# Readout tables among the chunk inputs, six weight halves on another engine, regrouped adaLN columns: one S5/convolution layer on one core

## The chip, the core and the metric

The kernel runs on one core of one Trainium2 chip. The metric is the device time of one execution in microseconds (us); a smaller one is better. Engines are named as in the profile: PE is TensorE (matmuls), DVE is VectorE, ACT is ScalarE, POOL is GpSimd, and SP is the queue that issues most DMAs.

## The reference, cut to what matters

One layer over 1024 latent tokens with 1024 channels and a prefix of 256 context tokens. adaLN gives shift, scale and gate vectors (six of 1024 channels). Two token mixers run side by side, a bidirectional diagonal state space model (S5) with a GLU, and a short gated convolution; they are merged by sigmoid gates. A gated MLP with a 3x3 depthwise convolution follows.

```python
h  = modulate(rmsnorm(x, norm1_g), sh1, sc1)
p  = h @ w_in
y_a = s5_branch(p[..., :512], pc[..., :512], ...)      # scan over chunks, readout, then z * sigmoid(z @ glu_w + glu_b)
y_b = b_gate * depthwise_conv1d(c_gate * x_val, sconv_w)
merged = gate_a * (y_a @ proj_a) + gate_b * (y_b @ proj_b)
x  = x + g1 * (merged @ w_out)
h2 = modulate(rmsnorm(x, norm2_g), sh2, sc2)
x  = x + g2 * conv_ffn(h2, ...)
```

## The kernel before

Matmuls in float32 precision are made of three passes: each operand is split in a high half (a ScalarE copy, `whi`, `ybh`, `woh`) and a low half (a subtraction, `wlo`, `ybl`, `wol`), and `mm3` adds three products (lines 211 to 213). `weight` (line 190) loads a 128x1024 block into `raw` (two buffers), makes `whi` on ScalarE (line 199) and `wlo` on VectorE, or on the engine given in `lo_eng` (line 202); whi and wlo have two buffers each. PSUM has two buffers of 128x1024 for such matmuls (`mm`) and a few small ones (`ax`).

The S5 branch works on 160 chunks of 8 tokens (32 of the context, 128 latent), in 32 groups, eight to a block m:
- `chunk_inputs(m)` (line 617) loads U and multiplies it by the tables W1 into the states XS, with three ScalarE copies for each of six small PSUM tiles. Then level 0 of the scan is done for block m, in three parts (`advance`, line 587, four VectorE steps a part at lines 603 to 606). Its temporaries lie in the pool bp, on the right side of SBUF.
- `build_w2(sb)` (line 631) makes one of eight readout tables of four groups: six VectorE steps (lines 637 to 642) into W2 (one buffer), two DMAs to Yd (line 644), four ScalarE copies into Bk, eight matmuls (`ax_K`, line 651) and a copy to Kt (line 653).
- `kernel_table` (line 655) makes the diagonal part K0 (matmuls at line 660, a VectorE step at line 662), writes Kt and K0 to Kd (lines 665, 666, 669), and copies Kd into Yd with 16 DMAs (line 672).
- `chunk_scan` (line 608) does levels 1 to 4 upwards, then the top, then levels 4 to 0 downwards, for groups 0 to 15 and then 16 to 31, on VectorE.
- `readout(sb)`, 16 of them: loads of `wt`, copies S of XS on ScalarE and VectorE (lines 786, 787), matmuls (lines 790 to 792), a gelu and DMAs to Zd.

The convolution: `conv_unit` for m = 0 to 3 with three `gate_matmul` each (mm_c, mm_x, mm_b, 48 matmuls each). The product of c and x goes to `cx` (one buffer), the three taps to `cv` (one buffer; lines 701 to 703), times mm_b (line 708), then the split to `ybh`, `ybl` in the pool yp. yp is opened on the right side when the pools bp and tb are closed (after line 740).

Then `branch_b(d)` for d = 0 to 7: gate 24 + d (48 matmuls, mm_gb, sigmoid at line 812), a projection (24 matmuls, mm_pb) and their product on VectorE (line 820). For d = 0 to 3 the readouts are issued between (0, 6, 6 and 4); before d = 4 the pool of XS is closed. From d = 4 on, three adaLN columns follow each branch: `mod_cols(n)` (line 845) loads 128 rows of 1024 and does one dot product on VectorE (line 849). Then z, gate 16, four GLU projections, the split to y_a, and branch a: gates 17 to 23 and proj_a (mm_ga, mm_pa; sigmoid at line 812, product at line 913), with the other twenty columns between, five for each of d = 1 to 4. `load_wout(k)` (line 897) loads a block of w_out into a `raw` buffer, multiplies it by g1b on GpSimd (line 900), and splits it.

What sets the order: the program's order is only a priority. Each engine's instructions are put in order when the kernel is built, by a simulated timeline of the program; on the chip each engine and each queue then goes strictly in that order. SBUF of a closed pool can be used again when its last reader is done. `issue_after` puts an instruction behind a given one on the same engine, as in

```python
    def held(eng):
        ins = hold.get(eng)
        return tc.issue_after(ins.ins) if ins is not None else nullcontext()
```

Of the kernel before, what the change touches and what calls it, by code (L numbers as in the profile page):

```python
# [22 lines left out]
P = 128  # L23
# [132 lines left out]
def layer_kernel(es: ExitStack, tc, I, out):  # L156
# [451 lines left out]
    def chunk_scan(gs, t1, t2, cap):  # L608

        for lv in range(1, NLV):  # L610
            advance(gs, lv, (2 << lv) - 1, t1, t2, cap)
        for c in range((2 << NLV) - 1, NC - 1, 1 << NLV):
            advance(slice(gs.start, gs.stop), NLV, c, t1, t2, cap, c)
        for lv in reversed(range(NLV)):
            advance(gs, lv, NCC - 1 + (1 << lv), t1, t2, cap, NC - 2)
# [15 lines left out]
    def build_w2(sb):  # L631
        g0 = sb * 4
        W2 = kp2.tile([P, 4, 2, L, H], F32, name=f"W2_{g0}", tag="W2")
        tmp = kp2.tile([P, 4, L, H], F32, name=f"W2t_{g0}", tag="W2t")
        e = [tview(E2[i], g0, 4) for i in range(2)]
        eng = dve
        eng.tensor_tensor(W2[:, :, 0], e[0], bview(Cr, g0, 4), op=ALU.mult)
        eng.tensor_tensor(tmp, e[1], bview(nCi, g0, 4), op=ALU.mult)
        eng.tensor_tensor(W2[:, :, 0], W2[:, :, 0], tmp, op=ALU.add)
        eng.tensor_tensor(W2[:, :, 1], e[0], bview(nCi, g0, 4), op=ALU.mult)  # L640
        eng.tensor_tensor(tmp, e[1], bview(Cr, g0, 4), op=ALU.mult)
        eng.tensor_tensor(W2[:, :, 1], W2[:, :, 1], tmp, op=ALU.subtract)
        for q in range(2):
            sync.dma_start(Yd[2 * sb + q][:, :, 0:2, :], W2[:, 2 * q:2 * q + 2].rearrange("p g r l h -> p g r (l h)"))
        pk = ax_tile([P, P], f"K{sb}")
        for i, b in enumerate((Br2, Bi2)):
            act.activation(Bk[i][0:64, :, 0:H], b[0:64, g0:g0 + 4], AF.Copy)
            act.activation(Bk[i][64:128, :, H:2 * H], b[64:128, g0:g0 + 4], AF.Copy)
        for g in range(4):
            for i in range(2):  # L650
                pe.matmul(pk[32 * g:32 * g + 32, :], Bk[i][:, g, :], W2[:, g, i].rearrange("p l h -> p (l h)"),
                          start=(i == 0), stop=(i == 1))
        act.activation(Kt[:, sb, :], pk, AF.Copy)

    def kernel_table():
        for m in range(MS):
# [5 lines left out]
            dve.scalar_tensor_tensor(K0[:, m, :], ident, dsk[:, m:m + 1], pk, op0=ALU.mult, op1=ALU.add)  # L662
        for q in range(4):
# [3 lines left out]
        for q in range(8):  # L667
            kg = Kd.rearrange("(m q) h i o -> q h m (i o)", q=8)[q]
            sync.dma_start(kg[:, :, 7 * H:8 * H], K0[16 * q:16 * q + 16, :, 16 * q:16 * q + 16])
# [61 lines left out]

    for m in range(MS):
        chunk_inputs(m)
        if m + 2 < MS:
            build_w1(2 * m + 4)
            build_w1(2 * m + 5)
        for g0, n in ((0, 3), (3, 3), (6, 2)):
            t1, t2 = (bp.tile([P, 512], F32, name=f"q{i}_{m}_{g0}", tag=f"T1_{i}") for i in range(2))
            advance(slice(8 * m + g0, 8 * m + g0 + n), 0, 1, t1, t2, 512)
    hold.clear()  # L740
# [4 lines left out]
    for sb in range(8):  # L745
        build_w2(sb)
# [7 lines left out]
    for gq in range(2):  # L754
        t1, t2 = (qp.tile([P, SEQ], F32, name=f"q{i}{gq}", tag=f"q{i}") for i in range(2))
        chunk_scan(slice(16 * gq, 16 * gq + 16), t1, t2, SEQ)
# [52 lines left out]
    def gate(m, key):  # L809
        psg = gate_matmul(m, key, pool_e)  # L810
# [4 lines left out]
    def branch_b(d):  # L815
        sg = gate(24 + d, f"gb{d}")
        if d % 2 == 0:
            conv["pw"] = weight(I["proj_b"][d // 2], pool_e)
# [33 lines left out]
    for d in range(MA, KT):  # L852
        branch_b(d)
        for n in range(3):
            mod_cols(16 + (d - MA) * 3 + n)
# [16 lines left out]
    sgd = {0: gate(16, "ga0")}  # L872
    for m in range(MS):
# [23 lines left out]
    def load_wout(k, src):  # L897
        raw = wp.tile([P, D], F32, name=f"raw_o{k}", tag="raw", bufs=2)
        sync.dma_start(raw, I["w_out"][k * P:(k + 1) * P, :])
        pool_e.tensor_tensor(raw, raw, g1b, op=ALU.mult)  # L900
# [5 lines left out]
    for d in range(KT):  # L906
# [8 lines left out]
        for n in range(28 + 5 * (d - 1), min(48, 28 + 5 * d)) if d else ():  # L915
            mod_cols(n)
# [277 lines left out]
```

## Time and profile before

| | us |
|---|---|
| median of 3 runs (lowest, highest) | 1476.52 (1476.14, 1478.03) |
| profiled execution | 1478.21 |
| span in its profile | 1476.4 |

| engine | busy us | share of the span |
|---|---|---|
| PE | 1401.2 | 95% |
| DVE | 973.5 | 66% |
| ACT | 539.6 | 37% |
| POOL | 508.0 | 34% |

A group's row names line, engine, operation, output <- input, shapes and count. A wait names the engine and line that waited and the instruction that ended the wait, as the profile infers it: if the named one had long been done, it was another, often a DMA. A start time is in us from the start of the span. Starts of neighbouring matmuls show their pace better than their durations, which overlap.

### The profile page before, as it was taken

To read this page: it belongs to the slowest core of one execution; us is meant where nothing else is said; L and a number is where in the kernel's file an instruction comes from. 1 tells how busy PE (TensorE), PEld (TensorE's weight loads), DVE (VectorE), ACT (ScalarE), POOL (GpSimd) and SP (SyncE) were. 2 spreads that over 40 slices of the span, in tenths; PEclk is the share of its full clock that TensorE was granted. 3 is DMA by queue.
4 is the path that set the end of the run, shared out by engine and by line. 5 is a ranking of instruction groups with operands and counts; after the bars stand their busy time and mean duration, and the time that the engine had idled before them with its cause. 6 is when DMAs were issued, how large, how long until landed. Compare 5 with 4: busy or idle time off the path is not lost. (4 is left out here: it accounts for less than half of the span.)

```text
span 1476.4 us, 16962 instructions
## 1 busy us (share of the span) xinstructions
PE 1401.2 (95%) x6488; PEld 1144.8 (78%) x6488; DVE 973.5 (66%) x1427; ACT 539.6 (37%) x760; POOL 508.0 (34%) x220
## 2 busy tenths in 40 slices
PE   6999978979999989999999999999999999998997
PEld 4787856768877767778878888888888887887885
DVE  6865789992143665037658878778787787349554
ACT  5645762215523411125433333323323342424332
POOL 0000000111123334550035554654555555645453
PEclk9999988989999998999999999999999999999999
DMA  9513211246674265133211111111111115434331
GB/s 327 196 50 95 78 41 60 78 114 184 210 206 117 79 213 142 58 106 122 87 42 51 43 57 44 47 54 44 57 43 44 57 45 191 140 96 141 109 107 57
DMA packets 82577, 148.71 MB, mean 101 GB/s; under 512 B 22336, under 2 KB 51264, under 8 KB 82496
## 3 DMA queue, kind: packets, MB, share of 16 engines
q1 hardware_dynamic: 79616, 137.90, 30.3%
q10 hardware_dynamic: 2880, 9.73, 1.9%
q8 instruction: 51, 0.84, 0.2%
q14 instruction: 30, 0.25, 0.0%
HBM read 129.80 MB, written 19.90 MB: 101 GB/s over the span
## 5 line engine op out<-in xcount | busy, mean ns | idle before, releaser
L202 POOL TENSOR_TENSOR wlo<-raw,whi 128x1024 fp32r<-128x1024 f32 x114 | 293.1, 2575 | 741.7 <-ACT whi L199 587.8
L1034 DVE SCALAR_TENSOR_TENSOR acc<-mm_up,cw,acc 128x945 f32<-128x945 f32 (+2 forms) x308 | 375.0, 1222 | 100.3 <-POOL acc L1026 91.5
L199 ACT ACTIVATE whi<-raw 128x1024 fp32r<-128x1024 f32 x126 | 133.6, 1060 | 499.6 <-issue 167.8
L213 PE MATMUL mm_up<-h2hi,wlo 128*128 128x512 f32 x704 | 273.8, 389 | 0.5 <-POOL wlo L202 0.5
L212 PE MATMUL mm_up<-h2lo,whi 128*128 128x512 f32 x704 | 274.0, 389 | 0.0
L211 PE MATMUL mm_up<-h2hi,whi 128*128 128x512 f32 x704 | 273.5, 389 | 0.4 <-DVE h2hi L969 0.4
L213 PEld LDWEIGHTS mm_up<-h2hi,wlo 128*128 128x128 f32 x704 | 132.2, 188 | 28.4 <-POOL wlo L202 0.9
L211 PEld LDWEIGHTS mm_up<-h2hi,whi 128*128 128x128 f32 x704 | 132.1, 188 | 28.0 <-DVE h2hi L969 0.7
L212 PEld LDWEIGHTS mm_up<-h2lo,whi 128*128 128x128 f32 x704 | 132.2, 188 | 27.3
L211 PE MATMUL mm_dn<-whi,fhd 128*128 128x512 f32 x308 | 119.5, 392 | 6.0 <-DVE x1r L1122 4.5
L212 PE MATMUL mm_dn<-wlo,fhd 128*128 128x512 f32 x308 | 120.7, 392 | 2.5 <-POOL wlo L202 2.5
L213 PE MATMUL mm_dn<-whi,fld 128*128 128x512 f32 x308 | 120.2, 391 | 0.0
L1026 POOL TENSOR_TENSOR acc<-acc,side 128x960 f32<-128x960 f32 x44 | 100.5, 2283 | 0.0
L207 DVE TENSOR_TENSOR fld<-f,fhd 128x512 fp32r<-128x512 f32 x44 | 57.6, 1323 | 53.5 <-ACT fhd L206 53.5
L849 DVE CUSTOM_DVE_ANT_0 mw<-mw,sc 128x1024 f32<-128x1024 f32 x32 | 54.1, 1699 | 47.1 <-DMA mw<-in_mod_wT_dram 42.5
L211 PEld LDWEIGHTS mm_dn<-whi,fhd 128*128 128x128 f32 x308 | 58.2, 189 | 18.9 <-DVE x1r L1122 4.9
L212 PEld LDWEIGHTS mm_dn<-wlo,fhd 128*128 128x128 f32 x308 | 58.3, 189 | 15.6 <-POOL wlo L202 3.5
L213 PEld LDWEIGHTS mm_dn<-whi,fld 128*128 128x128 f32 x308 | 58.2, 189 | 11.9
L196 DVE TENSOR_TENSOR raw<-raw,g2b 128x1024 f32<-128x1024 f32 x22 | 44.4, 2016 | 32.6 <-DMA raw<-in_ffn_w_down_dram 32.6
L211 PE MATMUL mm_ga<-hhi,whi 128*128 128x512 f32 x128 | 51.1, 400 | 11.4 <-ACT whi L199 11.4
L211 PE MATMUL mm_gb<-hhi,whi 128*128 128x512 f32 x128 | 51.6, 403 | 7.7 <-ACT sggb L812 7.7
L1045 POOL TENSOR_TENSOR f<-f,acc 128x1024 f32<-128x1024 f32 x22 | 53.4, 2426 | 10.1 <-DVE acc L1034 10.1
(323 smaller groups left out, 2655.7 us busy)
## 6 DMA issues: line engine op xcount, KB each, us to landing
raw<-in_ffn_w_up_dram SPq DMA_DIRECT2D x44, 512.0 KB
raw<-in_ffn_w_down_dram SPq DMA_DIRECT2D x44, 512.0 KB
mw<-in_mod_wT_dram SPq DMA_DIRECT2D x32, 512.0 KB
raw<-in_w_in_dram SPq DMA_DIRECT2D x28, 512.0 KB
wt<-Yd SPq DMA_DIRECT2D x16, 384.0 KB
mt<-in_mod_wT_dram SPq DMA_DIRECT2D x8, 512.0 KB
mn<-in_mod_nat_dram SPq DMA_DIRECT2D x8, 512.0 KB
Yd<-W SPq DMA_DIRECT2D x16, 256.0 KB
```

The source lines that it names most:

```text
L196: dve.tensor_tensor(raw, raw, scale, op=ALU.mult)
L199: act.activation(hi, raw, AF.Copy)
L202: (lo_eng or dve).tensor_tensor(lo, raw, hi.bitcast(F32), op=ALU.subtract)
L207: return dve.tensor_tensor(lo, src, hi.bitcast(F32), op=ALU.subtract)
L211: pe.matmul(ps, lh, rh, start=first, stop=False)
L212: pe.matmul(ps, lh, rl, start=False, stop=False)
L213: pe.matmul(ps, ll, rh, start=False, stop=last)
L849: dve.tensor_tensor_reduce(out=mw, in0=mw, in1=sc2, scale=1.0, scalar=0.0, op0=ALU.mult, op1=ALU.add, accum_out=modc[:, n:n + 1])
L1026: pool_e.tensor_tensor(acc[:, 1:, :], acc[:, 1:, :], side[:, 1:, :], op=ALU.add)
L1034: dve.scalar_tensor_tensor(acc[:, r0:r1, c0:c1], u[:, r0 + dr:r1 + dr, c0 + dc:c1 + dc], cw[:, m, i:i + 1], acc[:, r0:r1, c0:c1], op0=ALU. ...
L1045: pool_e.tensor_tensor(f[k], f[k], v, op=ALU.mult)
```

## The change

The diagonal table comes first, ahead of the chunk inputs. The tables 0 to 3 are built behind the chunk inputs of blocks 0 to 3, their matmuls one block later; tables 4 to 7 follow. Level 0 is done with the chunk inputs for blocks 0 and 1 only, and in `chunk_scan` for groups 16 to 31. Every step of the scan is put behind the last VectorE step of table 4. `hold` keeps its other entries, of instructions long issued by then. The low halves of gates 24 to 27 and of proj_b 0 and 1 are made on VectorE instead of GpSimd. The 32 adaLN columns are 9 behind branch b, 6 behind gate 16 and 17 in branch a, instead of 12 and 20. For w_out blocks 0 to 2, `raw` is a tile beside g1b, and the product is on VectorE.

```diff
@@ -605,9 +605,9 @@
             dve.tensor_tensor(dst, dst, a1, op=ALU.add)
             dve.tensor_tensor(dst, dst, a2, op=ALU.add)
 
-    def chunk_scan(gs, t1, t2, cap):
-
-        for lv in range(1, NLV):
+    def chunk_scan(gs, lv0, t1, t2, cap):
+
+        for lv in range(lv0, NLV):
             advance(gs, lv, (2 << lv) - 1, t1, t2, cap)
         for c in range((2 << NLV) - 1, NC - 1, 1 << NLV):
             advance(slice(gs.start, gs.stop), NLV, c, t1, t2, cap, c)
@@ -639,9 +639,13 @@
         eng.tensor_tensor(W2[:, :, 0], W2[:, :, 0], tmp, op=ALU.add)
         eng.tensor_tensor(W2[:, :, 1], e[0], bview(nCi, g0, 4), op=ALU.mult)
         eng.tensor_tensor(tmp, e[1], bview(Cr, g0, 4), op=ALU.mult)
-        eng.tensor_tensor(W2[:, :, 1], W2[:, :, 1], tmp, op=ALU.subtract)
+        hold[f"w2{sb}"] = eng.tensor_tensor(W2[:, :, 1], W2[:, :, 1], tmp, op=ALU.subtract)
         for q in range(2):
             sync.dma_start(Yd[2 * sb + q][:, :, 0:2, :], W2[:, 2 * q:2 * q + 2].rearrange("p g r l h -> p g r (l h)"))
+        return lambda: inner_table(sb, W2)
+
+    def inner_table(sb, W2):
+        g0 = sb * 4
         pk = ax_tile([P, P], f"K{sb}")
         for i, b in enumerate((Br2, Bi2)):
             act.activation(Bk[i][0:64, :, 0:H], b[0:64, g0:g0 + 4], AF.Copy)
@@ -652,7 +656,7 @@
                           start=(i == 0), stop=(i == 1))
         act.activation(Kt[:, sb, :], pk, AF.Copy)
 
-    def kernel_table():
+    def diagonal_table():
         for m in range(MS):
             pk = ax_tile([P, P], f"K0{m}")
             gs = slice(8 * m, 8 * m + 8)
@@ -660,13 +664,15 @@
                 pe.matmul(pk, b[:, gs, :].rearrange("p g h -> p (g h)"), cc[:, gs, :].rearrange("p g h -> p (g h)"),
                           start=(i == 0), stop=(i == 1))
             dve.scalar_tensor_tensor(K0[:, m, :], ident, dsk[:, m:m + 1], pk, op0=ALU.mult, op1=ALU.add)
+        for q in range(8):
+            kg = Kd.rearrange("(m q) h i o -> q h m (i o)", q=8)[q]
+            sync.dma_start(kg[:, :, 7 * H:8 * H], K0[16 * q:16 * q + 16, :, 16 * q:16 * q + 16])
+
+    def kernel_table():
         for q in range(4):
             kg = Kd.rearrange("(s q) h i o -> q h s (i o)", q=4)[q]
             sync.dma_start(kg[:, :, 8 * H:15 * H], Kt[32 * q:32 * q + 16, :, 0:7 * H])
             sync.dma_start(kg[:, :, 0:7 * H], Kt[32 * q + 16:32 * q + 32, :, H:8 * H])
-        for q in range(8):
-            kg = Kd.rearrange("(m q) h i o -> q h m (i o)", q=8)[q]
-            sync.dma_start(kg[:, :, 7 * H:8 * H], K0[16 * q:16 * q + 16, :, 16 * q:16 * q + 16])
         for j in range(L):
             for q in range(2):
                 sync.dma_start(Yd.rearrange("s (h j) q w o -> j q w s h o", j=L)[j, q, 2],
@@ -729,21 +735,28 @@
     for t in Bk:
         pool_e.memset(t, 0.0)
 
+    diagonal_table()
+    late = None
     for m in range(MS):
         chunk_inputs(m)
+        if late:
+            late()
         if m + 2 < MS:
             build_w1(2 * m + 4)
             build_w1(2 * m + 5)
-        for g0, n in ((0, 3), (3, 3), (6, 2)):
+        late = build_w2(m)
+        for g0, n in ((0, 3), (3, 3), (6, 2)) if m < 2 else ():
             t1, t2 = (bp.tile([P, 512], F32, name=f"q{i}_{m}_{g0}", tag=f"T1_{i}") for i in range(2))
             advance(slice(8 * m + g0, 8 * m + g0 + n), 0, 1, t1, t2, 512)
-    hold.clear()
+    hold.pop("dve")
     es_w.close()
     es_t.close()
     es_m = ExitStack()
     yp = pool("yp", stack=es_m, side="right")
-    for sb in range(8):
-        build_w2(sb)
+    for sb in range(MS, 8):
+        late()
+        late = build_w2(sb)
+    late()
     kernel_table()
     es_k2.close()
     es_u.close()
@@ -753,7 +766,8 @@
     qp = pool("qp", stack=es_q)
     for gq in range(2):
         t1, t2 = (qp.tile([P, SEQ], F32, name=f"q{i}{gq}", tag=f"q{i}") for i in range(2))
-        chunk_scan(slice(16 * gq, 16 * gq + 16), t1, t2, SEQ)
+        with held("w24"):
+            chunk_scan(slice(16 * gq, 16 * gq + 16), 1 - gq, t1, t2, SEQ)
     es_q.close()
 
     def ytile(key, m):
@@ -807,7 +821,7 @@
         return ps
 
     def gate(m, key):
-        psg = gate_matmul(m, key, pool_e)
+        psg = gate_matmul(m, key, None if 24 <= m < 28 else pool_e)
         sg = sgp.tile([P, SEQ], F32, name=f"sg{key}", tag="sg")
         act.activation(sg, psg, AF.Sigmoid)
         return sg
@@ -815,7 +829,7 @@
     def branch_b(d):
         sg = gate(24 + d, f"gb{d}")
         if d % 2 == 0:
-            conv["pw"] = weight(I["proj_b"][d // 2], pool_e)
+            conv["pw"] = weight(I["proj_b"][d // 2], None if d < 4 else pool_e)
         psp = proj_matmul(conv["pw"], d % 2, yb[0], yb[1], f"pb{d}")
         dve.tensor_tensor(mb[d], psp, sg, op=ALU.mult)
 
@@ -851,8 +865,8 @@
 
     for d in range(MA, KT):
         branch_b(d)
-        for n in range(3):
-            mod_cols(16 + (d - MA) * 3 + n)
+        for n in range(16 + 9 * (d - MA) // MA, 16 + 9 * (d - MA + 1) // MA):
+            mod_cols(n)
     es_ps.close()
     mm_order.insert(0, pool("ps_mm1", space=PSUM))
     es_ps = ExitStack()
@@ -870,6 +884,9 @@
 
     zh, zl = ysplit("z")
     sgd = {0: gate(16, "ga0")}
+    NM = 16 + 9 + 6
+    for n in range(16 + 9, NM):
+        mod_cols(n)
     for m in range(MS):
         if m % 2 == 0:
             wt = weight(I["glu_w"][m // 2], pool_e)
@@ -895,9 +912,10 @@
     wout = []
 
     def load_wout(k, src):
-        raw = wp.tile([P, D], F32, name=f"raw_o{k}", tag="raw", bufs=2)
+        raw = (wo.tile([P, D], F32, name=f"raw_o{k}", tag="xr", bufs=2) if k < 3 else
+               wp.tile([P, D], F32, name=f"raw_o{k}", tag="raw", bufs=2))
         sync.dma_start(raw, I["w_out"][k * P:(k + 1) * P, :])
-        pool_e.tensor_tensor(raw, raw, g1b, op=ALU.mult)
+        (dve if k < 3 else pool_e).tensor_tensor(raw, raw, g1b, op=ALU.mult)
         hi, lo = (src.tile([P, D], F32R, name=f"wo{t}{k}", 
                           **({"tag": "sg"} if src is sgp else {"tag": f"y{t}{k % MS}", "bufs": 1})) for t in ("h", "l"))
         split(hi, lo, raw)
@@ -912,7 +930,7 @@
         sg = sgd.pop(d)
         dve.tensor_tensor(sg, ps, sg, op=ALU.mult)
         pool_e.tensor_tensor(mb[d], mb[d], sg, op=ALU.add)
-        for n in range(28 + 5 * (d - 1), min(48, 28 + 5 * d)) if d else ():
+        for n in range(NM + 5 * (d - 1), min(48, NM + 5 * d)) if d else ():
             mod_cols(n)
         if 2 <= d < 4:
             load_wout(d - 2, wo)
```

## Rows read from the trace of the kernel before

**Rows 1.** Waits of PE, whole span: waiting line <- what ended it: us, times, longest.
```profile
PE mm_ga L211 <- ACT whi L199: 11.4, 2, 8.0
PE ax_K L651 <- DVE W L639: 8.9, 1, 8.9
PE mm_gb L211 <- ACT sggb L812: 7.7, 1, 7.7
...
PE ax_K L651 <- ACT whi L199: 5.0, 1, 5.0
...
PE mm_pb L211 <- DVE mb L820: 2.6, 1, 2.6
```

**Rows 2.** Windows by stage: busy us of each engine, granted clock, DMA share, GB/s.
```profile
core 0: us, PE busy (x) PEld busy (x) DVE busy (x) ACT busy (x) POOL busy (x), PEclk, DMA share, GB/s
125.00:203.50 78.50, 76.69 (x418) 65.69 (x417) 55.04 (x84) 57.63 (x92) 0.00 (x0) 1.00 0.23 70
203.50:226.00 22.50, 8.51 (x48) 6.31 (x48) 22.50 (x33) 9.15 (x20) 0.00 (x0) 0.71 0.23 70
203.50:330.00 126.50, 104.79 (x518) 81.04 (x518) 121.57 (x190) 30.79 (x60) 9.62 (x3) 0.89 0.29 83
460.00:510.00 50.00, 49.25 (x214) 39.77 (x213) 27.88 (x13) 27.95 (x19) 18.08 (x5) 1.00 0.14 42
510.00:600.00 90.00, 77.43 (x314) 61.41 (x313) 52.86 (x54) 14.40 (x16) 40.42 (x15) 0.92 0.57 175
```

**Rows 3.** PE's timeline behind stall B: start, us; 12 matmuls lie between the first two.
```profile
316.70 0.79 PE L211 MATMUL mm_gb<-hhi,whi 128*128 128x512 f32 x1 [7.72 <-ACT sggb L812]
...
322.39 0.39 PE L212 MATMUL mm_gb<-hlo,whi 128*128 128x512 f32 x1
322.62 0.40 PE L213 MATMUL mm_gb<-hhi,wlo 128*128 128x512 f32 x1
```

**Rows 4.** ACT's timeline around the stalls, idle time before in brackets.
```profile
213.85 1.06 ACT L206 ACTIVATE ybh<-cv 128x1024 fp32r<-128x1024 f32 x1 [6.05 <-DVE XS L606]
...
225.33 1.03 ACT L694 ACTIVATE cx<-mm_c 128x1024 f32<-128x1024 f32 x1 [5.72 <-DVE cv L703]
...
314.32 1.28 ACT L812 ACT_TABLE_LOAD   x1 [8.88 <-DVE XS L606]
...
593.93 1.06 ACT L206 ACTIVATE woh<-raw_o 128x1024 fp32r<-128x1024 f32 x1 [10.55 <-POOL raw_o L900]
```

**Rows 5.** DVE's timeline, table and scan steps between 209 and 330 us.
```profile
209.80 0.67 DVE L639 TENSOR_TENSOR W<-W,W2t 128x512 f32<-128x512 f32 x1
...
213.28 0.47 DVE L606 TENSOR_TENSOR XS<-XS,q 128x320 f32<-128x320 f32 x1
...
302.15 2.54 DVE L606 TENSOR_TENSOR XS<-XS,q 128x320 f32<-128x320 f32 x1
...
328.58 1.23 DVE L606 TENSOR_TENSOR XS<-XS,q 128x1024 f32<-128x1024 f32 x1
```

**Rows 6.** SP's queue: issue start, us of issuing, line, destination <- source.
```profile
309.23 3.66 SPq L669 DMA_DIRECT2D Kd<-K  x8
...
542.19 0.38 SPq L899 DMA_DIRECT2D raw_o<-in_w_out_dram  x1
544.60 5.01 SPq L847 DMA_DIRECT2D mw<-in_mod_wT_dram  x2
549.70 0.38 SPq L194 DMA_DIRECT2D raw<-in_w_in_dram  x1
```

**Rows 7.** The table tile W: duration ns min/median/max, first and last start.
```profile
L639 DVE TENSOR_TENSOR W<-W,W2t x8: 673/682/1769, 128.3 to 297.6; 128x512 f32<-128x512 f32 x8
```

**Rows 8.** Line 202, the weights' low halves, by engine, same columns.
```profile
L202 POOL TENSOR_TENSOR wlo<-raw,whi x114: 2357/2406/6788, 278.7 to 1440.2; 128x1024 fp32r<-128x1024 f32 x114
L202 DVE TENSOR_TENSOR wlo<-raw,whi x12: 1206/1218/1226, 61.2 to 265.8; 128x1024 fp32r<-128x1024 f32 x12
```

**Rows 9.** Line 790, the readouts' first matmul of three, same columns.
```profile
L790 PE MATMUL ax_Y<-S,wt x64: 270/275/348, 338.5 to 399.9; 128*128 128x128 f32 x64
```

## The prediction

> **What bounds the kernel now.** TensorE is busy nearly everywhere, so I first read what its matmuls wait for, line by line [rows 1]. Three places hold almost all of the idle time between 200 and 600 us that this change can touch, and two lesser ones go with them. Stall A (about 211 to 226 us): matmuls of the readout tables (ax_K) wait 5.0 and 8.9 us. Stall B (309 to 317 us): gate 1 of branch b waits 7.7 us for the sigmoid of gate 0. Stalls D and E (547 to 555 and 592 to 596 us): gates of branch a wait 11.4 us together, 8.0 in D and so 3.4 in E, for a weight's high half. Stall C (453 to 456 us): a projection waits 2.6 us for a product on VectorE. Sum: 13.9 + 7.7 + 2.6 + 11.4 = 35.6 us.
>
> Then the windows by stage [rows 2]: up to 203.5 us VectorE has 78.5 - 55.0 = 23.5 us to spare; from there to 330 us it is busy 121.6 of 126.5 us, while TensorE loses 14 us of the 22.5 in stall A. After an idle stretch the matmuls also come slower [rows 3]: behind stall B 13 of them start in 5.69 us, one every 0.44, and from 322.39 us one every 0.23; the granted clock is at its 1.2 GHz level first and at 2.4 GHz then. That is 13 x 0.21 = 2.7 us. I take 2 us behind each of the other four stalls (an estimate from this one, lower because three of them are shorter), so 10.7 us in all, and 46.3 us are there to win.
>
> Last the chains behind the stalls. A: ScalarE holds the split of y_b (ybh) until 213.85 us [rows 4], just after the last level-0 step (128x320, 213.28 us) on VectorE [rows 5]. That step uses a tile of the pool bp, in whose place the pool yp of y_b is opened; I infer that this memory is what is waited for. Behind ybh stand its low half, the next unit's cv, its two taps, then the copy of mm_c at 225.33 us [rows 4], and only then is a PSUM buffer free for mm_x. So the table matmuls are where TensorE waits, but the memory is why. B: the sigmoid starts at 314.32 us [rows 4], after the eight DMAs from K0, issued from 309.23 us for 3.66 us [rows 6]; sg probably lies where the table pool kp2 was. D: on the SP queue raw_o of w_out (542.19 us), two adaLN loads (544.60) and then the gate's weight (549.70) stand in line [rows 6], and raw_o takes one of the two raw buffers. E: the high half stands on ScalarE behind woh, at 593.93 us, which waited 10.55 us for the product raw_o x g1b on GpSimd [rows 4].
>
> **The change, part by part.** *Tables early.* A table is six VectorE steps of 0.68 us [rows 7], 4.1 us, two DMAs, 16 TensorE instructions and five small ScalarE copies. All counts stay. Tables 1 to 3 (12.3 us) now fall into the 23.5 spare us before 203.5; in their place level 0 of blocks 2 and 3 leaves the chunk inputs. So stall A's memory is free once block 3's last chunk matmul is done. I put that at 200 us, 13.8 before 213.85; the chain that ended at 226.4 (225.33 + 1) then ends near 212, and the matmuls of three more tables and the diagonal, done earlier, keep TensorE busy past 210. Bounds: 0 us left of A, or the whole chain's 4 us above that; I take 2 us left. If VectorE's spare time were not there, the tables would cost their own 12.3 us on the chain.
>
> *Diagonal early.* Eight short DMAs move ahead of the U loads on SP: 3.7 us at worst for the first chunk input [rows 6]. TensorE has convolution work there, so I cost it at nothing; without that cover it is 3.7 us. B's wait is gone if the last table is done before gate 0 ends. Tables after the first came every (297.6 - 209.8) / 6 = 14.6 us [rows 5, 7]; four left after 203.5 end near 262 us, and gate 0 now ends near 285.
>
> *The scan.* It starts behind table 4 instead of beside tables 1 to 7. Its VectorE work after 203.5 us: minus 12.3 (tables), minus about 7 (12 level-0 steps between 0.47 and 0.8 us), minus 1.4 (diagonal), plus 12.6 (level 0 of the second half as 12 steps of 864 elements, 1.05 us each, between the 320- and 1024-element rows [rows 5]). Queued behind the held steps are only later scan steps; all convolution steps may pass them. The entries kept in hold name instructions long done and cost nothing.
>
> *Weight halves.* Four gates and two proj_b weights, six halves, take 1.2 us on VectorE where GpSimd took 2.4 [rows 8]; about five of them and two products, 8.5 us, fall before the scan's end. Against that, each of the three GpSimd halves in this stretch stretched a VectorE step beside it: 302.15 us shows 2.54 for 0.47 us, 2.1 us [rows 5], and one table step 1.77 for 0.68, 1.1 us [rows 7]; with 1.1 for the third, 4.3 us come back. Net scan end: -12.3 - 7 - 1.4 + 12.6 + 8.5 - 4.3 = -3.9, so 326 instead of 329.8 us [rows 5].
> The Trainium skill (SBUF — State Buffer, Who interferes with whom) says that of a VectorE step with two SBUF inputs and a GpSimd step that reads SBUF, the later one blocks until the first ends. By that rule up to 3 x 2.4 = 7.2 us would come back and the scan would end at 323 us; the rows show less than a full block.
>
> *Readouts.* They run from the scan's end to 399.9 us [rows 9], 70 us for 16, with TensorE only interleaved. From 326 us they end at 396. Without A and B TensorE is done with projection 0 at 308.8 - 15.9 = 293 us, and has until it needs the memory that the readouts free: five gates and projections (72 matmuls x 0.23 = 16.4 us each, 82) and the readouts' own 21 us, so work until 396 us. The two just meet. I take 4 us lost here; bounds 0 and 20 (rival 1).
>
> *adaLN columns.* 32 dots and loads before and after: 12, 20 become 9, 6, 17. The nine end with the column that the first row write needs, and the next six are held behind the z splits. So no load is late in front of VectorE's projection product, and C goes, 4.6 us. The six lie in the z and GLU stage; VectorE was busy 28 of 50 us there [rows 2], and I cost them at nothing; the chain of z to the first proj_a waits at most for one dot, 1.2 us.
>
> *w_out rows 0 to 2.* They leave the raw ring for a buffer beside g1b, three loads keep their number, and the product goes from GpSimd to VectorE (3 x 1.2 us, VectorE busy 53 of 90 us from 510 to 600 us [rows 2]). D's weight has its buffer earlier and three fewer column loads ahead in all; E's woh no longer waits for a late load. Together 15.4 us; the loads on SP still wait in turn for dots, so 5 us may stay; bounds 0 and all.
>
> **Sum.** 46.3 - 2 - 4 - 5 = 35.3 us. The profiled execution took 1478.2 us (1.8 around its span), so 1442.9; the median of the runs is 1.7 lower, so 1441 us.
>
> **Rivals.** *1. Scan and readouts bind.* The tables have one W2 buffer; should tables 3 and 4 keep the 14.6 us spacing after 203.5, the scan starts some 20 us later and ends near 346. Then A and B give 26 - 20 = 6 us: 1476.5 - 6 - 4.6 - 10.4 = 1455. For it: VectorE had 5 idle us in 126.5 [rows 2]. Against: spare time before 203.5. *2. The queue, not the buffer, makes D and E.* Then column loads block as before: 1476.5 - (46.3 - 15.4 - 6) = 1452. For it: 544.60 stands in front of 549.70 [rows 6]. With both, 1466. *3. Slower: table matmuls in front of the convolution on TensorE.* It runs in order; if each of the eight tables stops it as in A, (5.0 + 8.9) / 2 = 7 us and 2 for the clock, that is 72 us against 46: 1502. It decides from five tables on. Against: the last five tables of before stop it nowhere. *4. The change does not do what it says.* If the order worked out at build time puts the tables after the chunk inputs anyway, all but the column part stays, and the time is within 0.2% (3 us, about what a measurement can tell).
>
> **Chances.** Forecast 0.53, rival 1 0.18, rival 2 0.16, rival 4 0.06, rival 3 0.07. Faster 0.53 + 0.18 + 0.16 and a little of the fourth, 0.88; same 0.05; slower 0.07. The range goes from all 46 us won and 2 more (1428) to both first rivals together (1464).
>
> **What would show it.** Right: no wait over 3 us of ax_K or mm_x around 205 to 226; ybh of unit 0 near 200; three tables' VectorE steps before 203.5; the last Kd DMA before gate 0 ends; no wait at gate 1; scan end near 326; no mm_ga wait over 3 us. Wrong: a wait of the first readout matmul or of gates 5 to 7 (rival 1), mw loads in front of a late weight (2), ax_K waits between 125 and 205 (3).

## The result and the profile after

The changed kernel takes 1457.25 us (median of 4 runs, 1454.36 to 1459.63) against 1476.76 for the kernel before on the same chip: ratio 0.9866, 95% interval 0.9847 to 0.9885. It is faster by 19.5 us; the forecast was 35.3. The profiled execution took 1457.23 us, its span is 1455.4.

The waits of TensorE over the whole span of the changed kernel, in the columns of [rows 1] (two longer ones, of ax_cr and mm_dn, stand in both kernels alike and are left out):

```profile
PE mm_ga L213 <- POOL wlo L202: 4.1, 2, 3.2
PE ax_Y L804 <- DMA wt<-Yd: 2.9, 2, 2.7
PE mm_glu L212 <- DVE zl L207: 2.8, 3, 2.0
...
PE mm_x L211 <- DVE cx L699: 2.3, 1, 2.3
```

The entries of [rows 1] are gone or under 1 us: the waits of ax_K for tables, of gate 1 for a sigmoid, of a projection for a product, of two gates for a high half. What stands in their place is small, 3.2 us at the longest, for a gate's low half. So why not 35 us? The list holds only idle time, wait by wait; it does not show where the work stands later than it could. For that I set the sigmoids of the gates side by side. Branch b's gates 0 to 7 and branch a's 0 to 7 are the same 16 steps in both kernels.

| us | before | after | change | forecast |
|---|---|---|---|---|
| start to sigmoid b0 (stalls A, B) | 315.6 | 293.8 | -21.8 | -24.3 |
| b0 to b7 (readouts) | 138.2 | 150.4 | +12.2 | +4.0 |
| b7 to a1 (z, GLU, stall C) | 55.2 | 56.8 | +1.6 | -4.6 |
| a1 to a7 (stalls D, E) | 117.6 | 104.9 | -12.7 | -10.4 |
| span | 1476.4 | 1455.4 | -21.0 | -35.3 |

The two ends came out near the forecast, the two middle stages cost 14.4 us more than it said. The busy time of three stretches shows where; first the kernel before, then the changed one, in the columns of [rows 2]:

```profile
190.00:230.00 40.00, 25.11 (x136) 19.86 (x136) 35.00 (x54) 23.80 (x41) 0.00 (x0) 0.79 0.13 40
...
360.00:400.00 40.00, 40.00 (x235) 34.78 (x234) 10.00 (x20) 19.43 (x35) 4.78 (x2) 1.00 0.69 208
400.00:430.00 30.00, 30.00 (x135) 24.64 (x134) 11.53 (x14) 10.53 (x10) 7.20 (x3) 1.00 0.64 213
```

```profile
190.00:230.00 40.00, 35.74 (x201) 28.05 (x200) 24.23 (x33) 27.19 (x51) 0.00 (x0) 0.96 0.21 66
...
360.00:400.00 40.00, 35.33 (x212) 30.57 (x211) 11.12 (x20) 21.39 (x36) 5.59 (x3) 1.00 0.64 188
400.00:430.00 30.00, 28.35 (x134) 24.04 (x133) 5.57 (x10) 10.76 (x18) 2.40 (x1) 0.83 0.74 235
```

From 190 to 230 us TensorE gained 10.6 us (stall A), and VectorE, the engine that has the scan still to do, now idles 40 - 24.23 = 15.8 us. From 360 to 430 TensorE, which never stopped before, idles 6.3 us, and its clock falls to a mean of 0.83 in the second stretch, which is up to 0.17 x 28.4 = 4.8 us more. Counted from the sigmoid of gate 1, behind the slow matmuls of stall B, to that of gate 7, the stage is 12.9 us longer: TensorE idles 6.3 us against 1.9, and is busy 129.0 us against 120.6 with the same gates, projections and readouts. The clock is up to 4.8 of these 8.4 us; where the others lie is open. VectorE's timeline of the changed kernel links the two:

```profile
188.84 0.49 DVE L606 TENSOR_TENSOR XS<-XS,q 128x320 f32<-128x320 f32 x1
195.20 0.69 DVE L637 TENSOR_TENSOR W<-keep,keep 128x512 f32<-128x512 f32 x1 [5.87 <-PE ax_K L655]
...
207.25 1.23 DVE L202 TENSOR_TENSOR wlo<-raw,whi 128x1024 fp32r<-128x1024 f32 x1 [7.98 <-ACT whi L199]
...
224.50 0.82 DVE L603 TENSOR_TENSOR q<-XS,PR 128x640 f32<-128x640 f32 x1
...
353.54 1.23 DVE L606 TENSOR_TENSOR XS<-XS,q 128x1024 f32<-128x1024 f32 x1
...
411.64 2.36 DVE L834 TENSOR_TENSOR mb<-mm_pb,sggb 128x1024 f32<-128x1024 f32 x2 [0.38 <-ACT S L800]
```

Table 2 (counted from 0) starts at 195.20 only, because the one W2 buffer is held until TensorE has done the matmuls of table 1, which are issued one block later: 5.9 us of idle time. Then VectorE stands 8.0 us behind a weight half that ScalarE delivers late. The scan starts at 224.5 us and ends at 354.8, not at 326. The readouts run to 419.0 (399.9 before, [rows 9]). The first product of the second half of mb waits for the last readout's copies out of XS (411.64): its memory, I infer from the code, is that of XS and the readouts. Until then, by the code, both PSUM buffers of the projections are taken, and gate 6 of branch b cannot start: its sigmoid comes 42 us after that of gate 5, where 15 to 17 are usual.

VectorE from 203.5 us to the scan's end, to set beside the third line of [rows 2]:

```profile
203.50:354.80 151.30, 147.51 (x703) 117.27 (x703) 133.84 (x188) 39.90 (x64) 4.95 (x2) 0.99 0.28 80
```

It works 133.8 us and idles 17.5; before, it worked 121.6 us and idled 4.9 to 330 us. So the later scan end is made of both, idle time and work.

ScalarE's timeline in the stretch of stall A:

```profile
205.26 0.88 ACT L629 ACTIVATE XS<-ax_X 64x384 f32<-64x384 f32 x1
206.16 1.06 ACT L199 ACTIVATE whi<-raw 128x1024 fp32r<-128x1024 f32 x1
...
210.31 1.06 ACT L206 ACTIVATE ybh<-cv 128x1024 fp32r<-128x1024 f32 x1
```

The split of y_b runs at 210.31 us (213.85 in [rows 4]) with no idle time in front of it: it no longer waits for VectorE, but stands behind ScalarE's own copies of the chunk states. Even so mm_x starts at 218.8 us and not at 226.5.

### The profile page after: what moved, and what is told of

It is laid out like the page before. It is cut to its first block, busy times and chain, and to the rows that moved or that the text cites. A ratio compares the mean times of both kernels' runs of the same rounds, so it can differ in the third digit from the quotient of the medians.

```text
span 1455.4 us, 16944 instructions
## 1 busy us (share of the span) xinstructions
PE 1399.7 (96%) x6488; PEld 1144.0 (79%) x6488; DVE 979.1 (67%) x1424; ACT 535.2 (37%) x758; POOL 477.5 (33%) x211
## 5 line engine op out<-in xcount | busy, mean ns | idle before, releaser
L202 POOL TENSOR_TENSOR wlo<-raw,whi 128x1024 fp32r<-128x1024 f32 x108 | 269.8, 2502 | 758.6 <-ACT whi L199 750.9
L212 PE MATMUL mm_dn<-wlo,fhd 128*128 128x512 f32 x308 | 120.6, 392 | 2.5 <-POOL wlo L202 2.5
L213 PE MATMUL mm_ga<-hhi,wlo 128*128 128x512 f32 x128 | 50.7, 396 | 4.1 <-POOL wlo L202 4.1
L213 PE MATMUL mm_o<-woh,ml 128*128 128x512 f32 x128 | 50.8, 398 | 1.1 <-DVE ml L207 1.1
```

What stands on the lines that cost most here:

```text
L202: (lo_eng or dve).tensor_tensor(lo, raw, hi.bitcast(F32), op=ALU.subtract)
L212: pe.matmul(ps, lh, rl, start=False, stop=False)
L213: pe.matmul(ps, ll, rh, start=False, stop=last)
```

## The experiments

Times are medians. The kernel before came out at 1472.0, 1473.9, 1471.9 and 1472.1 us beside the four groups of runs, so I ran the changed kernel again among them: 1455.34 us (ratio 0.9895, 0.9866 to 0.9924). The runs are compared with that one. The stages are those of the table above; the scan column is the start of its last step, the readouts go from the first to the last of their first matmuls.

| run | us | start to b0 | b0 to b7 | b7 to a1 | a1 to a7 | scan | readouts |
|---|---|---|---|---|---|---|---|
| after_again | 1455.34 | 291.9 | 151.1 | 56.1 | 104.7 | 351.5 | 356.6 to 417.8 |
| e1_no_hold | 1452.85 | 296.1 | 143.2 | 56.5 | 104.2 | 341.9 | 351.3 to 414.2 |
| e11_now_nohold | 1453.65 | 297.9 | 144.9 | 53.9 | 104.5 | 340.1 | 348.9 to 408.8 |
| e12_silu_first | 1452.66 | 297.2 | 145.7 | 55.6 | 103.9 | 339.5 | 348.3 to 409.0 |
| e14_zd_act | 1456.77 | 293.9 | 150.4 | 56.6 | 104.4 | 353.6 | 358.7 to 418.1 |
| e16_zd_wt3_nohold | 1449.23 | 297.6 | 138.5 | 56.2 | 103.6 | 343.4 | 352.8 to 396.4 |
| e3_level0 | 1447.44 | 300.2 | 136.6 | 55.9 | 105.5 | 333.4 | 343.2 to 401.4 |
| e17_block3_wt3 | 1444.71 | 293.0 | 140.0 | 55.5 | 106.0 | 340.5 | 352.0 to 396.0 |
| e8_halves_pool | 1459.58 | 292.3 | 154.6 | 56.5 | 104.6 | 350.9 | 355.8 to 420.9 |
| e5_wout_old | 1465.79 | 291.9 | 149.2 | 59.3 | 115.9 | 351.6 | |
| e7_cols_old | 1471.05 | 293.1 | 149.8 | 67.4 | 111.5 | 352.8 | |
| e6_wout_alone | 1470.03 | 315.6 | 137.0 | 52.3 | 114.6 | 328.6 | |

**The changed kernel again.**

> The changed kernel, unaltered, beside the other runs of this group. The runs so far set kernels measured in different groups side by side, and the kernel before came out 4.7 us lower in the second group (1472.0 against 1476.8). If that was a shift of every kernel, the changed kernel comes out near 1452-1454 us here, ratio 0.9866, and removing the hold was worth nothing; if it belongs to stalls that only the kernel before has, it comes out at 1457 us, and removing the hold was worth 4-5 us.

It lies between: 1455.34, and the kernel before at 1473.89. Two of its six executions took 1463.3 and 1466.1 us. Removing the hold, below, is then worth 2.5 us, within what the scatter allows.

**The hold of the scan.** First theory: the scan's late start, put there by the hold behind table 4, is what costs.

```diff
-        with held("w24"):
+        with nullcontext():
```

> The changed kernel without the hold: the scan may go to VectorE as soon as its inputs are there, among the last four readout tables. Theory 1 (the late scan costs the missing gain): the scan's first step moves from 224.5 us to about 205, its last L606 step from 353.5 to 333-345, the last readout matmul from 419 to 400-410, and TensorE's idle stretch between 393 and 419 us shrinks: 1444-1450 us. Rival (the readouts are paced by their own loads whatever the scan does, or the scan is no shorter because VectorE has the same work either way): the scan's end moves by less than 5 us or the readouts' end does not follow it, 1455-1459 us.

1452.85 us, between the two ranges. The scan ends 10 us sooner, but the readouts only 4, and TensorE is 4.3 us later at b0: scan steps stand in front of table steps on VectorE, and ax_K waits 4.3 us for one. Of 7.9 us won behind, about half is lost in front. The hold is not the main cause, it moves the loss.

**Tables' matmuls at once.** The W2 buffer was to come free sooner:

```diff
-        late = build_w2(m)
+        build_w2(m)()
```

(and the delayed calls left out, the hold too).

> The changed kernel without the hold, and with each table's matmuls put straight behind its six VectorE steps instead of one block of chunk inputs later, so that the one W2 buffer comes free sooner. Theory 1 with the buffer as its cause: VectorE's idle of 5.9 and 8.0 us between 189 and 207 us goes, tables 2 to 4 start 8-15 us sooner, the scan ends at 325-335 us and the readouts near 400: 1441-1447 us, 2-5 us below the run without the hold alone. Rival (VectorE was only waiting for work that it had to do anyway, or TensorE now waits on the tables in front of the convolution): TensorE shows new waits for W2 of 5 us or more near 175-215 us and the time is that of the run without the hold alone or above it, 1448-1460 us.

1453.65 us, as without the hold alone: the scan's end moved by 1.8 us more, gates 0 to 7 took no less. The buffer did come free: tables 2 to 4 start 9 to 12 us sooner than in the changed kernel. But VectorE still idles 11.4 us of the 40 in the stretch of stall A, as in the run without the hold alone (11.2):

```profile
190.00:230.00 40.00, 33.86 (x170) 25.92 (x168) 28.64 (x41) 28.32 (x49) 0.00 (x0) 0.87 0.21 66
```

So the one W2 buffer is not what leaves that stretch empty. In this run a gate waited 4.4 us for a sigmoid that stood on ScalarE behind the silu of c, whose load stood behind the last stores of the readouts. The next run was to take that away, with the load of c and its silu issued ahead of the z loads:

> The run without the hold and with each table's matmuls straight behind its VectorE steps, and besides the load of c and its silu issued ahead of the last z load. Theory (the queue behind the last readout's stores holds up the silu, and the silu the sigmoid of gate 30): the wait of 4.4 us for that sigmoid before TensorE's gate 30 goes, the adaLN columns start 4-6 us sooner, and with them the halves of z in front of the first GLU matmuls: 1445-1450 us, 4-7 us below the same kernel with the silu late. Rival (the columns are bound by the loads that share the queue, not by when the first starts): within 2 us of it, 1452-1455 us.

1452.66 us: the wait shrank from 4.4 to 3.1 and the time did not move beyond the scatter. The theory is not tested by it: the load of c was issued at 418.18 us instead of 418.28, because it waited 5.5 us for the last store of the readouts in its new place too, and the silu still ran in front of the sigmoid.

**Level 0 back among the chunk inputs.** The tables stay early and the scan held.

```diff
-        for g0, n in ((0, 3), (3, 3), (6, 2)) if m < 2 else ():
+        for g0, n in ((0, 3), (3, 3), (6, 2)):
-            chunk_scan(slice(16 * gq, 16 * gq + 16), 1 - gq, t1, t2, SEQ)
+            chunk_scan(slice(16 * gq, 16 * gq + 16), 1, t1, t2, SEQ)
```

> The changed kernel with level 0 of the scan done among the chunk inputs for all four blocks, as before, instead of for the first two. The tables stay early. Theory (wait A was the memory of y_b, which the last level-0 step frees): the first high half of y_b waits for the last level-0 step again, TensorE idles 8-12 us before mm_x near 215-230 us (2.3 us in the changed kernel), and the scan after it is some 10 us shorter, so that the time is 1455-1463 us. Rival (wait A was VectorE's and ScalarE's backlog, which the early tables keep): TensorE's wait there stays under 4 us, and with the scan 5-10 us earlier the time is 1448-1454 us.

1447.44 us, 7.9 below the changed kernel, outside its scatter and under both ranges: of the parts undone so far, the level-0 steps that the change took out of the chunk inputs cost most. One window, one row of ScalarE and two of TensorE from this run:

```profile
190.00:230.00 40.00, 30.10 (x181) 22.89 (x181) 33.74 (x54) 29.09 (x56) 0.00 (x0) 0.87 0.21 66
```

```profile
214.86 1.06 ACT L206 ACTIVATE ybh<-cv 128x1024 fp32r<-128x1024 f32 x1 [2.66 <-DVE XS L606]
```

```profile
221.94 0.61 PE L655 MATMUL ax_K<-W,Bk 128*32 128x128 f32 x2 [5.70 <-DVE W L639]
225.53 1.10 PE L655 MATMUL ax_K<-W,Bk 128*32 128x128 f32 x14 [2.99 <-DVE W L642]
```

VectorE is busy 33.7 us of the 40 instead of 24.2: the 24 steps of level 0 of blocks 2 and 3 fill much of the time in which the changed kernel idles, and the scan ends 18 us sooner (from 203.5 us to its end VectorE works 121.6 us and idles 9.5). Gates 0 to 7 then take 136.6 us, no more than before. In front both theories are half right. The split of y_b does wait again for the last level-0 step (214.86 us against 208.3 in after_again), so the memory that this step holds (inferred, as in the prediction) was a cause of stall A; but TensorE waits where it did in the kernel before, at the table matmuls, because the table steps on VectorE stand behind level 0, and b0 comes 8.3 us later.

**How long the readouts take.** In every run but two, 58 to 65 us, wherever the scan ends. Two causes were possible: one queue, or two buffers.

```diff
-            sync.dma_start(Zd[m][q * H:(q + 1) * H].rearrange("h i c -> i h c"), Zt[:, g, :])
+            act.dma_start(Zd[m][q * H:(q + 1) * H].rearrange("h i c -> i h c"), Zt[:, g, :])
```

> The changed kernel with the stores of the readouts' results issued by ScalarE instead of SyncE, so that they no longer stand in the same queue as the loads of the next readouts. Theory (what is lost behind the scan is lost because sixteen readouts take 60 us through one queue, in which a store that waits for its gelu holds the next load up): from the first readout matmul (358.7 us) to the last (419.0) it takes 40-50 us instead of 60, the wait of TensorE before gate 30 falls from 13 us to under 5, and the time is 5-12 us below the changed kernel (1455.3): 1443-1450 us. Rival (the readouts are paced by the transfers or by their two buffers): 57-60 us again, 1453-1458 us.

It came out as the rival said: 59.4 us and no gain, though 32 stores left the queue. Then also three buffers, and no hold:

```diff
-        wt = rd.tile([P, 2, 4, P], F32, name=f"wt{sb}", tag="wt")
+        wt = rd.tile([P, 2, 4, P], F32, name=f"wt{sb}", tag="wt", bufs=3)
```

> The same, and the scan not held, and three buffers instead of two for the readouts' tables. Theory (both ends of the readout stage count: its start at the scan's end and its length): the scan ends near 342 us as in the run without the hold, the last readout falls before 395 us, TensorE has no idle stretch there, the adaLN columns start before 410 us, and the halves of z wait for nothing: 1438-1446 us. Rival (what is won in front of the columns is lost on the convolution's side, where the run without the hold lost 4 us): 1446-1452 us, no better than with the stores on ScalarE alone.

1449.23 us, the rival's range: the readouts take 43.6 us and gates 0 to 7 are back at 138.5, but the front loses 5.7 us, much as in the run without the hold. The table loads on SyncE's queue, first of the changed kernel, then of this run:

```profile
354.79 0.60 SPq L794 DMA_DIRECT2D wt<-Yd  x1
...
356.07 0.57 SPq L794 DMA_DIRECT2D wt<-Yd  x1
...
360.26 0.52 SPq L794 DMA_DIRECT2D wt<-Yd  x1
```

```profile
344.71 0.60 SPq L794 DMA_DIRECT2D wt<-Yd  x1
...
346.00 0.57 SPq L794 DMA_DIRECT2D wt<-Yd  x1
...
347.25 0.52 SPq L794 DMA_DIRECT2D wt<-Yd  x1
```

With two buffers the third load waits for the first readout's matmuls; with three it follows 1.25 us behind the second.

**Both causes together.** Level 0 early for three blocks, so that only the last block's, which stands in front of the tables, is left to the scan; the hold stays; three buffers.

```diff
-        for g0, n in ((0, 3), (3, 3), (6, 2)) if m < 2 else ():
+        for g0, n in ((0, 3), (3, 3), (6, 2)) if m < 3 else ():
-            chunk_scan(slice(16 * gq, 16 * gq + 16), 1 - gq, t1, t2, SEQ)
+            if gq:
+                advance(slice(24, 32), 0, 1, t1, t2, SEQ)
+            chunk_scan(slice(16 * gq, 16 * gq + 16), 1, t1, t2, SEQ)
```

> The changed kernel with level 0 of the scan done among the chunk inputs for three of the four blocks (only the last block's is left to the scan), and three buffers for the readouts' tables. Theory (VectorE's idle stretch of 16 us between 180 and 220 us is where the missing gain went; what fills it without standing in front of the tables that TensorE waits for is free): gate 24 ends near 292-296 us as in the changed kernel (300 with all four blocks), the scan ends near 332-345, the last readout falls before 395 us, gates 24 to 31 take 137-139 us as in the kernel before: 1441-1446 us. Rival (each microsecond of level 0 taken in early is lost in front of gate 24, as between the changed kernel and the run with all four blocks): 1446-1450 us.

1444.71 us, ratio 0.9811 (0.9787 to 0.9835), faster than both kernels: 10.6 us under the changed one, and in the theory's range. The readouts take 44 us with their stores on SyncE's queue, so the third buffer is enough for that. Its window of stall A, and the product that had waited until 411.64 us:

```profile
190.00:230.00 40.00, 35.59 (x195) 27.31 (x193) 29.13 (x42) 26.42 (x49) 0.00 (x0) 0.96 0.21 66
```

```profile
391.53 1.23 DVE L836 TENSOR_TENSOR mb<-mm_pb,sggb 128x1024 f32<-128x1024 f32 x1 [0.41 <-ACT S L802]
```

TensorE keeps the changed kernel's 35.6 us, VectorE does 4.9 us more, and the memory comes free 20 us sooner. How much three buffers give without the level-0 edit was not tried with the hold in place, and the 2.7 us between this run and the one with all four blocks lie within the scatter.

**The low halves.**

```diff
-        psg = gate_matmul(m, key, None if 24 <= m < 28 else pool_e)
+        psg = gate_matmul(m, key, pool_e)
-            conv["pw"] = weight(I["proj_b"][d // 2], None if d < 4 else pool_e)
+            conv["pw"] = weight(I["proj_b"][d // 2], pool_e)
```

> The changed kernel with the low halves of gates 24 to 27 and of the first two projection weights back on GpSimd. VectorE loses six steps of 1.22 us, 7.3 us in all, in the stretch in which it works on the scan. Theory (VectorE's load sets the scan's end there): the scan ends 5-8 us sooner, at 346-349 us, and the last readout with it, the GpSimd steps lengthen a few VectorE steps by 1-2 us each, and the time is 2-4 us lower than the changed kernel. Rival (the halves on GpSimd make TensorE wait for a low half of 2.4 us instead of 1.22, once per gate): 2-6 us higher, with waits for the low half of gb in the trace.

1459.58 us, 4.2 above the changed kernel here, 2.3 above its first median: that this part of the change helps is not shown beyond its scatter. VectorE loses 7.3 us of work and the scan ends 0.6 us sooner: the steps beside GpSimd swell. Seven GpSimd halves start before the scan's end, and beside each of them one VectorE step takes 2.0 to 2.2 us longer than others of its line and shape, 15.2 us in all; in the changed kernel there are two, 4.4 us. VectorE's and GpSimd's timelines of this run:

```profile
324.19 2.53 DVE L604 TENSOR_TENSOR q<-XS,PI 128x160 f32<-128x160 f32 x1
326.64 0.31 DVE L605 TENSOR_TENSOR XS<-XS,q 128x160 f32<-128x160 f32 x1
...
341.64 3.42 DVE L604 TENSOR_TENSOR q<-XS,AIx 128x1024 f32<-128x1024 f32 x1
```

```profile
324.03 2.51 POOL L202 TENSOR_TENSOR wlo<-raw,whi 128x1024 fp32r<-128x1024 f32 x1 [8.44 <-ACT whi L199]
...
340.52 3.46 POOL L202 TENSOR_TENSOR wlo<-raw,whi 128x1024 fp32r<-128x1024 f32 x1 [13.98 <-ACT whi L199]
```

A step of a shape that otherwise takes about 0.31 us, and that starts 0.16 us behind a GpSimd step, takes 2.53 and ends 0.18 us behind it. The waits for the low half of gb that the rival wanted are not among TensorE's longer ones; the first readout matmul waits 6.5 us for its table instead.

**w_out and the columns, each undone in the changed kernel, and w_out alone in the kernel before.**

```diff
-        raw = (wo.tile([P, D], F32, name=f"raw_o{k}", tag="xr", bufs=2) if k < 3 else
-               wp.tile([P, D], F32, name=f"raw_o{k}", tag="raw", bufs=2))
+        raw = wp.tile([P, D], F32, name=f"raw_o{k}", tag="raw", bufs=2)
-        (dve if k < 3 else pool_e).tensor_tensor(raw, raw, g1b, op=ALU.mult)
+        pool_e.tensor_tensor(raw, raw, g1b, op=ALU.mult)
```

> The changed kernel with the first three rows of the output weight loaded and scaled as before: through the ring of two raw buffers, scaled on GpSimd. Theory (the ring held the gate weights up): TensorE waits for a weight's high half again near 520-530 us and 575 us, 8 and 3.4 us as in the kernel before, and the time is 10-15 us above the changed kernel, 1467-1472 us. Rival (the waits D and E went because six adaLN columns left that stretch): at most 3 us above, 1457-1460 us.

1465.79 us, 10.5 above, just under the theory's range: a wait of 6.4 us and one of 1.6 for a gate's high half are back. Then the columns:

```diff
-        for n in range(16 + 9 * (d - MA) // MA, 16 + 9 * (d - MA + 1) // MA):
+        for n in range(16 + 3 * (d - MA), 16 + 3 * (d - MA + 1)):
...
-    NM = 16 + 9 + 6
-    for n in range(16 + 9, NM):
-        mod_cols(n)
+    NM = 28
```

> The changed kernel with the adaLN columns placed as before: twelve among the last convolution gates, none in front of the GLU, twenty behind. Theory 3 (moving six columns in front of the GLU only shifted time): the wait of about 5 us at the end of the convolution stage comes back, the stretch from the first GLU gate to the second loses the 7 us it gained, and the time is within 2 us of the changed kernel, 1455-1459 us. Rival (the regrouping was a gain of its own, as the prediction had it): 1461-1464 us.

1471.05 us, 15.7 above: both missed, the regrouping is worth over three times the 4.6 us that the prediction gave it. TensorE (two rows) and VectorE of this run:

```profile
468.42 0.80 PE L212 MATMUL mm_glu<-zl,whi 128*128 128x512 f32 x1 [9.18 <-DVE zl L207]
...
573.38 0.80 PE L211 MATMUL mm_ga<-hhi,whi 128*128 128x512 f32 x1 [7.30 <-ACT whi L199]
```

```profile
464.08 1.23 DVE L863 CUSTOM_DVE_ANT_0 mw<-mw,sc 128x1024 f32<-128x1024 f32 x1 [5.86 <-DMA mw<-in_mod_wT_dram]
```

Twelve columns stand in front of the last z halves on VectorE, most of them waiting for their loads, and hold them up until the GLU has waited 9.2 us at one matmul and 14.0 in all; that stage is 11.3 us longer. The column loads stand behind the readouts' last stores on SyncE's queue, so I read it that the columns are late where the readouts end late and TensorE is early; with nine in front, in the changed kernel, the longest such wait is 2.0 us. Behind a1 the run loses another 6.8 us, where a gate waits 7.3 us for its high half again, though w_out has its own buffers. And w_out alone:

> The kernel before, with one part of the change alone: the first three rows of the output weight through two buffers of their own, scaled on VectorE. Theory (the ring of raw buffers makes waits D and E): both waits for a weight's high half, 8.0 and 3.4 us, go or fall below 2, and the time is 9-14 us under the kernel before, ratio 0.990-0.994. Rival (the queue of column loads makes them): at least one stays at over 3 us and the ratio is 0.996-1.000.

1470.03 us, ratio 0.9977 (0.9964 to 0.9989): the rival's range, though only one of the two waits stays. Wait E is gone, D stays, moved by one gate. ScalarE and TensorE of this run, then ScalarE of the changed kernel:

```profile
569.11 1.06 ACT L206 ACTIVATE woh<-raw_o 128x1024 fp32r<-128x1024 f32 x1 [23.56 <-DVE modc L849]
570.07 1.04 ACT L199 ACTIVATE whi<-raw 128x1024 fp32r<-128x1024 f32 x1
```

```profile
571.16 0.80 PE L211 MATMUL mm_ga<-hhi,whi 128*128 128x512 f32 x1 [7.78 <-ACT whi L199]
```

```profile
553.15 1.06 ACT L206 ACTIVATE woh<-raw_o 128x1024 fp32r<-128x1024 f32 x1 [12.72 <-DVE modc L863]
554.12 1.04 ACT L199 ACTIVATE whi<-raw 128x1024 fp32r<-128x1024 f32 x1
```

The split of a w_out row waits on ScalarE for the last adaLN column (its place, I infer, is the columns' memory), and the gate's high half stands behind it. With 20 columns behind the GLU that is 569 us (571 in the changed kernel with the old columns), with 17 it is 553, and the gate waits no more for it. In the run with w_out as before the half waits for its own load instead, issued at 541.28 us, as it does at 549.70 in [rows 6]. So neither part does it alone: w_out alone gives 3.9 us, the columns without w_out leave 6.4 + 1.6 us of waits, both together gain 12.7 us in that stage.

## Why the prediction was right and wrong

- **Right: faster, and inside the range.** The time lies nearer to rival 1's 1455 than to the forecast's 1441, and the middle stages missed by 14.4 us. Stalls A and B: 21.8 us of 24.3. B is gone because the last table ends before gate 0. A is gone, but the split of y_b comes at 210.3 us and not at 200: ScalarE's copies of the chunk states stand in front, which my chain left out. No run puts the tables back behind the chunk inputs, so their share in A and B is read from the traces and not from an edit.
- **Wrong: the step "Net scan end", 326.** The scan ended 29 us later than I said. From 203.5 us on VectorE worked 16.2 us more than the sum leaves (133.8 against 121.6 - 3.9) and idled 12.5 us more (17.5 against 4.9), while the sum took its idle time as unchanged. Tables 1 to 3 were to fall before 203.5; table 3 starts at 208.4, because VectorE stood first behind the one W2 buffer and then behind a late weight half. Level 0 was taken out of a stretch with room and put into the scan, and 15.8 us of that stretch stood empty; that cost idle time there and work behind. And two GpSimd halves still fell beside the scan, with 4.4 us of swelling that the sum had taken out. The rest of the 16.2 was not separated. Putting level 0 back gave 7.9 us; three of its four blocks and a third buffer gave 10.6. This is rival 1, with the place right and the price not: 12.2 us instead of 20. Its sign, a wait at gates 5 to 7, came at gate 6; its reason, tables 14.6 us apart, did not, for tables 3 to 5 start 10.7 and 12.6 us apart. That the time came out 2 us from its 1455 is in part luck.
- **Wrong: the term of 4 us lost at the readouts.** It was worth 12.2. That they run "70 us for 16" with TensorE only interleaved was read as a given; two table buffers make it, 60 us from the first matmul to the last against 44 with three.
- **Wrong: the six columns "at nothing" and 4.6 us from C.** C's wait went, but the stage took 1.6 us more, not 4.6 less, 6.2 in all. TensorE waits there 2.8 us for low halves of z, which stand behind the columns on VectorE, and 2.1 for a weight's low half from GpSimd. Late readouts are at most a small part of it: where the readouts end at 396 us (e17) the stage still takes 55.5 us, against 52.3 in the kernel before with w_out alone, and TensorE waits 3.0 us at the GLU for a weight's low half from GpSimd (0.8 there). Why GpSimd is late in the new order was not separated.
- **Right in size, with half the cause: D and E.** 12.7 us for 10.4. I put D down to the queue and the ring of raw buffers, rival 2 to the queue alone. The late load is there, but behind it stands a second cause that I did not see: ScalarE at a w_out row until the last column is done. One part of the change takes the first away, the other the second, and each is needed: without the one 10.5 us are lost, without the other the gate waits 7.3 us.
- **The halves.** I priced them at +8.5 - 4.3 = 4.2 us of VectorE time; the run without them shows 0.6 us of scan, because 10.8 us of swelling come in for the 7.3 us that leave; VectorE idles 4.1 us less instead (9.0 against 13.1 us from 222 to 356). Three GpSimd steps were in my sum, where seven stand before the scan's end in that run, and the price per step was too low: the rows gave 1.1 to 2.1 us, the run 2.0 to 2.2. The rule that I weighed against the rows (the Trainium skill, SBUF — State Buffer, Who interferes with whom: the later of the two steps blocks until the first ends) fits both: in the three places of the kernel before, too, the VectorE step ended 0.35 to 0.68 us behind the GpSimd step (the one beside 302.15 us ran from 301.29 for 3.05 us). Two of the three lost only 1.1 us because they began with 1.2 us of the GpSimd step left.
- **Rivals 3 and 4** did not happen: no ax_K wait over 0.9 us, and the tables did move.

## What to carry to other kernels

Before moving work off an engine's busy stretch, ask what that engine will do in the stretch it leaves: steps taken out of a stretch with room leave idle time there, and come back on the path. Waits of the bounding engine show where it stops, not how much work it has ahead; compare stage lengths between the same marks, and look for the memory that ends a stage. A gain can need two parts at once, so undo each part in the changed kernel as well as adding it alone to the old one.

## What the runs showed of the hardware that I had not expected

A GpSimd step of 2.5 us held a VectorE step of about 0.31 us up to its own end (2.53 us), and one of 1.22 us became 3.42: the delay, 2.2 us in both, did not shrink with the size of the VectorE step. TensorE's granted clock fell to about its 1.2 GHz level behind a gap in the middle of dense work, in the changed kernel's readouts (windows of ten us each, columns of [rows 2]):

```profile
390.00:400.00 10.00, 6.35 (x45) 5.49 (x44) 1.94 (x4) 4.50 (x9) 2.35 (x1) 1.00 0.72 204
400.00:410.00 10.00, 9.02 (x39) 7.89 (x38) 2.41 (x6) 4.29 (x9) 0.00 (x0) 0.51 0.60 166
410.00:420.00 10.00, 9.33 (x53) 8.03 (x53) 3.16 (x4) 1.95 (x5) 0.00 (x0) 0.98 0.81 255
```

It had been busy 6.35 us in the ten before; the clock was 0.51 in the next ten, though TensorE was busy 9.0 of them. In the run with level 0 early, where it was busy 39.4 us of the 40 before 400 us, the clock stayed at 1.00.
